# Slots 520 instead of 512 elements long for the streamed operands of a decoder trunk

## The chip, the cores and the metric

The kernel runs on one core of one Trainium2 chip, in one launch. The metric is device time in microseconds. TensorE (PE) multiplies, VectorE (DVE), ScalarE (ACT) and GpSimd (POOL) do the elementwise work, and SyncE (SP) issues most of the loads. All operands of the products lie in SBUF, in tiles of 128 partitions. A place in SBUF is told below by its byte within a partition, as the built program has it, because every partition of a tile uses the same one.

## The reference

Two decoder layers on 1024 tokens of width 1024, all in float32. Cut to what matters:

```python
for i in range(2):
    shift_t, scale_t, gate_t, shift_c, scale_c, gate_c = split(silu(c) @ ada_w[i] + ada_b[i], 6)
    h = rmsnorm(x, norm_g[i, 0]) * (1.0 + scale_t) + shift_t
    y = gla_mixer(h, ...) if i == 0 else diff_mixer(h, ...)      # projections of h, mixing, @ w_o
    x = x + gate_t * y
    h = rmsnorm(x, norm_g[i, 1]) * (1.0 + scale_c) + shift_c
    x = x + gate_c * (square(relu(h @ mlp_w1[i])) @ mlp_w2[i])   # 1024 -> 4096 -> 1024
return rmsnorm(x, final_g)
```

Layer 0 mixes with gated linear attention (4 heads), layer 1 with differential softmax attention (8 heads).

## The kernel before

Activations are held transposed: 8 tiles of 128 features by 1024 tokens, and the tokens in two halves of `HT` = 512. Every float32 operand of a large product is kept as two parts, `hi` (rounded to float32r) and `lo` (the rest), made by `split` (L111). A product of two such operands is three matmuls on PE, in `mm3` (L115 to L118): weight hi with activation hi, weight hi with activation lo, weight lo with activation hi. In most products the weight part is the loaded operand (128 x 128, LDWEIGHTS in the trace, engine row PEld) and the activation part streams through, 512 columns at a time:

```python
pe.matmul(out=o, lhsT=lh, rhs=rh, start=start, stop=False)     # L116
pe.matmul(out=o, lhsT=lh, rhs=rl, start=False, stop=False)     # L117
return pe.matmul(out=o, lhsT=ll, rhs=rh, start=False, stop=stop)  # L118
```

`lhsT` is loaded, `rhs` streams. The streamed tiles that this document is about are these:

- `h`, the input of a projection or of the MLP, in the pool `hp`, which has 16 slots for each of two tags: `hhi` for the first parts (`h_hi`) and `hlo` for the second (`h_lo`). Before the first projection the same slots hold `xn` and `xT`, the input with tokens along the row.
- `hd`, the squared ReLU inside the MLP, in the pool `hid`, with four tags (`hd00`, `hd01`, `hd10`, `hd11`: half of the tokens, then first or second part) of four slots each.

The MLP is in `stretch`: for each of eight chunks of 512 inner features, 8 row groups (two halves of the tokens by four tiles of features) of 24 matmuls stream `h` into PSUM tiles `acc`, `hd` is made from them, and 192 matmuls stream `hd` into `acc` again, whose sums go to the residual `x` on DVE (L712). In the last chunk the second half is done in two pieces of 256 columns. In the MLP of layer 0, called the first MLP below, POOL also loads pieces of the adaLN weights of layer 1, DVE multiplies them, and PE adds them up with four transposes (L220) between two row groups; the MLP of layer 1, the second, has none of this. The output projections stream `h` as well (`acc`, `out_proj`), and so do the projections of the gated linear attention (`pq`, `pk` and `pr`). In the projections of the values there (`pv`) and of the whole differential attention (`pp`) the roles are swapped: a slice of `h` is loaded, and the weight streams, 256, 272 or 384 columns.

A slot is as long as its tile: 2048 bytes for 512 elements. The pools lie one behind the other, so slots of 2048 bytes keep the distance to a multiple of 256 that the first of them has. As built:

| tile | first byte of the first slot | step | bytes behind a multiple of 256 |
|---|---|---|---|
| weights, first and second parts | 19296, 41056 | 4352 | 96, each slice of them too |
| `h_hi` | 71520 | 2048 | 96 |
| `h_lo` | 104288 | 2048 | 96 |
| `hd` of the first MLP | 180256 | 2048 | 32 |
| `hd` of the second MLP | 153440 | 2048 | 96 |

The order of the pools `sm`, `tp`, `xp` and `hid` differs between the layers (`order` in `stretch`), which is why `hd` stands at two different places. The order of the instructions is set by the tile framework's scheduler, and in the two mixers PE's order is written out by hand (an agenda with lags).

Of the kernel before, what the change touches and what calls it, by code (L numbers as in the profile page):

```python
# [10 lines left out]
F32 = mybir.dt.float32  # L11
F32R = mybir.dt.float32r
# [9 lines left out]
P = 128  # L22
D = 1024
T = 1024
KT = D // P
HT = 512
FF = 4096
EPS = 1e-6
# [12 lines left out]

# How much other work of TensorE lies between a piece of work and one that needs its results: in
# rough microseconds of products (gated linear attention), in slots (differential attention).
GLA_LAG = dict(rank=1.09, decay=4.71, keys=3.36, score=4.04, out=7.24, step=2.16, turn=14.56, ada=30.5)
DIFF_LAG = dict(rotary=2.55, keys=1.95, turn=3, next=1.6, value=2, rms=2.66, norm=6.53)
DIFF_END = dict(turn=1.27, next=0.57, value=1.15, rms=1.1, norm=2)
DIFF_LEAD = 22
DIFF_RATE = {True: 2.0, False: 3.0}    # pieces of the output projection per slot, before and after its last operand


class Agenda:
    """Work that is put off until enough other work has been issued (`now` counts it)."""

# [16 lines left out]
def two_pi_parts():  # L70
    """2*pi cut into parts of four bits, so that a part times an integer below 2**20 is exact."""
    rest, parts = 2.0 * math.pi, []
    step = 2.0 ** -1
    while step > 2.0 ** -46:
        part = math.floor(rest / step) * step
        parts.append(part)
        rest -= part
        step /= 16.0
    return [p for p in parts if p]
# [3 lines left out]
def trunk(ctx: ExitStack, tc, a, out):  # L83
    nc = tc.nc
    pe, act, dve, pool = nc.tensor, nc.scalar, nc.vector, nc.gpsimd

# [1 line left out]
    const = ctx.enter_context(tc.tile_pool(name="const", bufs=1))  # L88
# [20 lines left out]

# [1 line left out]
    def split(hi, lo, src):  # L111
# [8 lines left out]
    def weight(src, shape, pinned=False):  # L120
        """Load a piece of a weight and split it into two parts of float32r."""
        raw = wraw.tile(shape, F32, name="raw", tag="raw")
        c0 = 0
        for part in src if isinstance(src, list) else [src]:
            c1 = c0 + part.shape[-1]
            i = nc.sync.dma_start(out=raw[:, :, c0:c1], in_=part)
            c0 = c1
            if pinned:
                in_order(i)
        hi = wsp.tile(shape, F32R, name="whi", tag="whi")  # L130
        lo = wsp.tile(shape, F32R, name="wlo", tag="wlo")
        split(hi, lo, raw)
        return hi, lo

    def wcols(w, c0, n, pinned=False):
        """Columns of a weight with its rows on partitions: [128, k, n]."""
        return weight(w.rearrange("(k p) n -> p k n", p=P)[:, :, c0:c0 + n], [P, KT, n], pinned)
# [5 lines left out]
    def new_half():  # L143
        return [(hp.tile([P, HT], F32R, name="h_hi", tag="hhi"), hp.tile([P, HT], F32R, name="h_lo", tag="hlo"))
                for _ in range(KT)]

    def rsqrt_cols(r, ms, scratch, n, scale=1.0 / D):
        """r = (ms * scale + eps) ** -0.5 for a few columns, with a Newton step."""
        m = scratch.tile([P, n], F32, name="rs_m", tag="rs_m")
        t = scratch.tile([P, n], F32, name="rs_t", tag="rs_t")  # L150
        dve.tensor_scalar(out=m, in0=ms, scalar1=scale, scalar2=EPS, op0=ALU.mult, op1=ALU.add)
        act.activation(out=t, in_=m, func=AF.Ln)
        act.activation(out=r, in_=t, func=AF.Exp, scale=-0.5)
        dve.tensor_tensor(out=t, in0=r, in1=r, op=ALU.mult)
        dve.tensor_tensor(out=t, in0=t, in1=m, op=ALU.mult)
        dve.tensor_scalar(out=t, in0=t, scalar1=-0.5, scalar2=1.5, op0=ALU.mult, op1=ALU.add)
        dve.tensor_tensor(out=r, in0=r, in1=t, op=ALU.mult)

    def broadcast(bc, cols, n):
        """bc[:, j*128:(j+1)*128] = cols[:, j] on every partition."""  # L160
        for j in range(n):
            pe.matmul(out=bc[:, j * P:(j + 1) * P], lhsT=cols[:, j:j + 1].broadcast_to([P, P]),  # L162
                      rhs=ident, start=True, stop=True)

    def norm_mod(x, half, h, gcols, shift, tmp, small, ps, cols=slice(0, HT), on_pool=()):
        """h = x / rms(x) * gcols + shift, in two parts, for the tokens cols of a half."""
        w = cols.stop - cols.start
# [30 lines left out]
    def ada_block(l, c0, n, raws, accs, ps, queue, tag="st", bufs=1):  # L198
        """mod[:, l, c0/128 ...] of n columns: products on VectorE, sum over partitions on PE."""
        ada_sums(l, c0, n, ada_products(l, c0, n, raws, accs, queue), ps, tag, bufs)  # L200
# [25 lines left out]
    def gscale(l, j):  # L226
        """norm_g * (1 + scale) of sub-layer j of layer l."""
        sc = mod[:, l, (3 * j + 1) * KT:(3 * j + 2) * KT]
# [7 lines left out]
    def gla_v(hd, i, pinned=False):  # L236
# [4 lines left out]

# [1 line left out]
    gla = ctx.enter_context(ExitStack())  # L243
    gp = gla.enter_context(tc.tile_pool(name="gp", bufs=1, space=PSUM, reuse_waits="tile"))
    gp2 = gla.enter_context(tc.tile_pool(name="gp2", bufs=1, space=PSUM, reuse_waits="tile"))
    win = a["gla_w_in"][0]
    xn = [hp.tile([P, HT], F32, name="xn", tag="hhi") for _ in range(KT)]
    xT = [hp.tile([P, HT], F32, name="xT", tag="hlo") for _ in range(KT)]
    h = [[(hp.tile([P, HT], F32R, name="h_hi", tag="hhi"), hp.tile([P, HT], F32R, name="h_lo", tag="hlo"))]
         for _ in range(KT)]  # L250

# [115 lines left out]
    def log_sigmoid(z, bias, tp, tag1, tag2):  # L367
        """min(z + b, 0) and log(1 + exp(-|z + b|)); their difference in place of the first."""
        t1 = tp.tile([P, HT], F32, name="ls1", tag=tag1)
# [8 lines left out]
    with gla as g:  # L378
# [49 lines left out]
        def decays(u, first=False):  # L428
            """Cumulated decays of a head inside each tile of 128 tokens, around its middle."""
            hd = u["hd"]  # L430
# [53 lines left out]
        def out_step(u, j):  # L484
            """The outputs of a tile of 128 tokens, and the state behind it."""
            hd, half, v, qi, ks = (u[n] for n in ("hd", "half", "v", "qi", "ks"))
# [46 lines left out]
        def unit(hd, half, ws):  # L533
            """The projections of a head for half of the tokens, in pieces of three products."""
            u = dict(hd=hd, half=half, v=[])
# [45 lines left out]
        with tc.tile_pool(name="xb", bufs=2, reuse_waits="tile") as xb:  # L581
# [7 lines left out]
            def second_half():  # L589
# [5 lines left out]
                for k in range(KT):  # L595
# [5 lines left out]
                    nc.sync.dma_start(out=xs[k, :, HT:T], in_=xc)  # L601
                    hi, lo = hp.tile([P, HT], F32R, name="h_hi", tag="hhi"), hp.tile([P, HT], F32R, name="h_lo", tag="hlo")
                    h[k].append((hi, lo))
# [22 lines left out]
        def stream():  # L626
            """The projections of all heads but the first unit's, and the first ones of the gates."""
            for hd in range(GLA_H):
# [46 lines left out]

# [1 line left out]
    def acc_mm():  # L677
        return mm.tile([P, HT], F32, name="acc", tag="mm")

    def out_proj(h, half, w_o, acc, done, ahead=False, ready=None):  # L680
        """The output projection of a mixer for half of the tokens, in pieces of three products; if
        it is ahead, the last tile of the rows comes at the end, on its own."""
        rows, ends = KT - 1 if ahead else KT, []
# [40 lines left out]
    def stretch(l, h, w_o, ada_todo, after, x=None):  # L724
        with ExitStack() as g:
# [31 lines left out]
            for c in range(FF // 512):  # L757
                ws = [wcols(w1, c * 512 + n * P, P) for n in range(4)]
                hd = [[None, None] for _ in range(4)]
                for half in range(2):  # L760
                    for n in range(4):
# [8 lines left out]
                        dve.tensor_tensor(out=r, in0=r, in1=r, op=ALU.mult)  # L770
                        hd[n][half] = [hid.tile([P, HT], F32R, name="hd", tag=f"hd{half}{i}") for i in range(2)]
                        split(hd[n][half][0], hd[n][half][1], r)
# [37 lines left out]

# [1 line left out]
    win = a["diff_w_in"][0]  # L812
    o = [[None, None] for _ in range(KT)]
    x = [[None, None] for _ in range(KT)]
    with ExitStack() as g:
# [15 lines left out]
        def projections():  # L831
            """The projections of all heads, in pieces of three products."""
            for hd in range(DIFF_H):
# [43 lines left out]
        def turn_qk(hd, half, qk, gi):  # L877
            """Queries as [hi; lo] and keys as [hi; hi] (and lo apart), with dimensions on partitions."""
            tr = dp.tile([P, HT], F32, name="tr", tag="tr", bufs=2)
# [80 lines left out]
        def turn_a(pair, j0):  # L960
            """Weights of two query tiles against two key tiles, with keys on partitions."""
            lastp = j0 == 2 * pair["pr"]
# [115 lines left out]
    def finish(half, cols, x, tp, sm, ps, acc_tile):  # L1078
        """The last norm with tokens on partitions, two tiles of tokens at a time."""
        if not grow:  # L1080
# [39 lines left out]
def diff_constants(tc, const, dc, pos, le, colsT):  # L1120
    """cos and sin of the rotary angles [128 tokens, 8 tiles, 8], -lambda, the sub-norm's gain and
    the causal mask (as an upper bound) of a diagonal block."""
    nc = tc.nc
# [64 lines left out]
```

## Time and profile before

| | before |
|---|---|
| median of 3 runs | 2598.0 us (2597.88 to 2598.4) |
| span of the profiled execution | 2596.7 us |
| PE busy | 2533.6 us, 98% of the span, 12551 matmuls |
| PEld, DVE, ACT, POOL busy | 81%, 57%, 35%, 7% |
| moved by DMA | 202.59 MB, mean 78 GB/s |

The span goes from the first to the last instruction of the one execution that was traced; the runs' own time is taken around the launch and lies 1.3 us above it. A matmul's busy time contains its passage through the array, which overlaps the next matmul, so that the busy times of PE's single instructions add up to more than its share of the span, and the distance from one start to the next is what a matmul costs in a row. Times in the rows below are from the start of the span.

### The profile page before, as it was taken

What the parts mean: (1) busy time and instruction counts of PE and PEld (TensorE: products, weight loads), DVE (VectorE), ACT (ScalarE), POOL (GpSimd) and SP (SyncE); (2) the same over time, 40 slices, a digit from 0 to 9 for tenths busy, and PEclk for the clock granted to TensorE, in tenths of its full rate; (3) what the DMA queues carried; (4) which work ended last, traced back from release to release, by engine and by line L of the source; (5) the groups of instructions that cost most, each with busy time, mean ns of one, the idle gap of its engine ahead of it and who ended that gap; (6) DMA issues with size and microseconds to landing.
All of it is one profiled execution on the core that took longest, in us unless ns stands there. A gap on an engine that the chain in (4) does not pass through costs nothing.

```text
span 2596.7 us, 32374 instructions
## 1 busy us (share of the span) xinstructions
PE 2533.6 (98%) x12551; PEld 2114.2 (81%) x12551; DVE 1481.8 (57%) x2872; ACT 915.4 (35%) x1849; POOL 181.0 (7%) x322
## 2 busy tenths in 40 slices
PE   7899999999999999999999999999999999999998
PEld 5788878888888888888888888887788888888887
DVE  7877786745355445337677777687743343334334
ACT  5645555422112211224455554554422122212222
POOL 2111110001011001000211111110000000000000
PEclk9999999999999999999999999999999999999999
DMA  8333364213133223113001111023311111111111
GB/s 279 120 112 114 119 206 147 81 42 113 50 121 97 93 69 110 41 47 102 25 29 33 34 33 33 23 78 114 114 41 57 41 55 43 50 48 49 49 41 65
DMA packets 224025, 202.59 MB, mean 78 GB/s; under 512 B 10426, under 2 KB 194912, under 8 KB 223872
## 3 DMA queue, kind: packets, MB, share of 16 engines
q1 hardware_dynamic: 209472, 156.33, 19.5%
q0 software_dynamic: 12992, 41.97, 5.2%
q8 instruction: 98, 1.61, 0.3%
q10 hardware_dynamic: 1408, 2.24, 0.2%
q14 instruction: 55, 0.45, 0.1%
HBM read 180.57 MB, written 19.92 MB: 77 GB/s over the span
## 4 chain that ended last, share of the span: by engine, by line
PE 87%; issue 5%; DVE 3%; DMA 2%; ACT 2%; POOL 0%; DVEq 0%; SPq 0%; POOLq 0%; ACTq 0%
PE acc L116 20%; PE acc L117 20%; PE acc L118 20%; PE pp L116 5%; PE pp L118 3%; PE pp L117 3%; DMA ada_raw<-in_ada_w 2%; PE at L966 1%; PE bc L162 1%; PE pr L116 1%; PE pr L117 1%; PE pr L118 1%; PE po L117 1%; PE po L118 1%; PE po L116 1%
## 5 line engine op out<-in xcount | busy, mean ns | idle before, releaser
L116 PE MATMUL acc<-h_hi,whi 128*128 128x512 f32 x1280 | 505.0, 395 | 1.9 <-DVE x L712 1.8
L117 PE MATMUL acc<-h_lo,whi 128*128 128x512 f32 x1280 | 500.5, 391 | 0.0
L118 PE MATMUL acc<-h_hi,wlo 128*128 128x512 f32 x1280 | 500.4, 391 | 0.0
L112 ACT CAST whi<-raw 128x1024 fp32r<-128x1024 f32 (+2 forms) x217 | 221.1, 1020 | 714.3 <-PE acc L117 667.0
L712 DVE SCALAR_TENSOR_TENSOR x<-acc,mod,x 128x512 f32<-128x512 f32 (+1 forms) x312 | 224.2, 722 | 366.4 <-PE acc L118 365.7
L116 PE MATMUL acc<-hd,whi 128*128 128x512 f32 (+1 forms) x1088 | 412.9, 380 | 1.3 <-DVE x L712 1.3
L118 PE MATMUL acc<-hd,wlo 128*128 128x512 f32 (+1 forms) x1088 | 412.7, 379 | 0.0
L117 PE MATMUL acc<-hd,whi 128*128 128x512 f32 (+1 forms) x1088 | 412.3, 379 | 0.0
L113 DVE TENSOR_TENSOR wlo<-raw,whi 128x1024 fp32r<-128x1024 f32 (+2 forms) x217 | 258.5, 1192 | 132.7 <-ACT whi L112 125.7
L116 PEld LDWEIGHTS acc<-h_hi,whi 128*128 128x128 f32 x1280 | 240.9, 188 | 55.2 <-issue 3.6
L118 PEld LDWEIGHTS acc<-h_hi,wlo 128*128 128x128 f32 x1280 | 241.2, 188 | 50.3
L117 PEld LDWEIGHTS acc<-h_lo,whi 128*128 128x128 f32 x1280 | 241.2, 188 | 47.9
L116 PEld LDWEIGHTS acc<-hd,whi 128*128 128x128 f32 x1088 | 204.5, 188 | 42.5 <-DVE x L712 1.8
L118 PEld LDWEIGHTS acc<-hd,wlo 128*128 128x128 f32 x1088 | 204.4, 188 | 40.7
L117 PEld LDWEIGHTS acc<-hd,whi 128*128 128x128 f32 x1088 | 204.3, 188 | 40.7
L770 DVE TENSOR_TENSOR relu<-relu 128x512 f32<-128x512 f32 x128 | 88.0, 688 | 206.0 <-ACT relu L769 205.9
L116 PE MATMUL pp<-whi,h_hi 128*128 128x384 f32 x512 | 199.4, 389 | 0.0
L118 PE MATMUL pp<-whi,h_lo 128*128 128x384 f32 x512 | 172.9, 338 | 0.0
L117 PE MATMUL pp<-wlo,h_hi 128*128 128x384 f32 x512 | 172.5, 337 | 0.0
L769 ACT ACTIVATE relu<-acc 128x512 f32<-128x512 f32 x128 | 75.8, 593 | 219.9 <-PE acc L118 219.9
L207 POOL DMA_DIRECT2D ada_raw<-in_ada_w x160 | 85.9, 537 | 867.0 <-DVE ada_acc L210 531.9
L112 ACT CAST hd<-relu 128x512 fp32r<-128x512 f32 x128 | 79.4, 621 | 158.3 <-DVE relu L770 158.2
(1760 smaller groups left out, 3806.5 us busy)
## 6 DMA issues: line engine op xcount, KB each, us to landing
raw<-in_mlp_w SPq DMA_DIRECT2D x128, 512.0 KB, 3.6
ada_raw<-in_ada_w POOLq DMA_DIRECT2D x160, 256.0 KB, 3.3
raw<-in_gla_w_in SPq DMA_DIRECT2D x24, 512.0 KB, 4.0
raw<-in_diff_w_in SPq DMA_DIRECT2D x64, 192.0 KB, 2.9
raw<-in_diff_w_o SPq DMA_DIRECT2D x17, 512.0 KB, 3.7
aw<-in_ada_w SPq DMA_DIRECT2D x16, 512.0 KB, 7.6
raw<-in_gla_w_o SPq DMA_DIRECT2D x16, 512.0 KB, 3.9
x<-xs SPq DMA_DIRECT2D x32, 256.0 KB, 4.6
```

The source lines that it names most:

```text
L112: act.copy(out=hi, in_=src)
L113: dve.tensor_tensor(out=lo, in0=src, in1=hi.bitcast(F32), op=ALU.subtract)
L116: pe.matmul(out=o, lhsT=lh, rhs=rh, start=start, stop=False)
L117: pe.matmul(out=o, lhsT=lh, rhs=rl, start=False, stop=False)
L118: return pe.matmul(out=o, lhsT=ll, rhs=rh, start=False, stop=stop)
L162: pe.matmul(out=bc[:, j * P:(j + 1) * P], lhsT=cols[:, j:j + 1].broadcast_to([P, P]), rhs=ident, start=True, stop=True)
L207: queue.dma_start(out=w, in_=a["ada_w"][l].rearrange("(k p) n -> p k n", p=P)[:, k:k + kk, c0:c0 + n])
L712: return dve.scalar_tensor_tensor(out=t, in0=psum, scalar=mcols(l, gate)[:, kt:kt + 1], in1=t, op0=ALU.mult, op1=ALU.add)
L769: act.activation(out=r, in_=pt, func=AF.Relu)
L770: dve.tensor_tensor(out=r, in0=r, in1=r, op=ALU.mult)
L966: pe.transpose(out=at[:, n * P:(n + 1) * P], in_=pair["es"][i][:, j * P:(j + 1) * P], identity=ident)
```

## The change

The slots with tag `hhi` and the slots of `hd` become 520 elements (2080 bytes) long. The tiles in them are still 512 wide: the last eight elements are never read or written. The slots of `h_lo` stay at 2048 bytes.

```diff
+PAD = 8
...
     def new_half():
-        return [(hp.tile([P, HT], F32R, name="h_hi", tag="hhi"), hp.tile([P, HT], F32R, name="h_lo", tag="hlo"))
-                for _ in range(KT)]
+        return [(hslot(F32R, "h_hi", "hhi"), hslot(F32R, "h_lo", "hlo")) for _ in range(KT)]
+
+    def hslot(dt, name, tag):
+        return hp.tile([P, HT + (PAD if tag == "hhi" else 0)], dt, name=name, tag=tag)[:, :HT]
...
-                        hd[n][half] = [hid.tile([P, HT], F32R, name="hd", tag=f"hd{half}{i}") for i in range(2)]
+                        hd[n][half] = [hid.tile([P, HT + PAD], F32R, name="hd", tag=f"hd{half}{i}")[:, :HT] for i in range(2)]
```

Three other places that take tiles of these tags (`xn`, `xT`, the first and the second half of layer 0's `h`) call `hslot` in the same way. Comments and docstrings are dropped too, which only shifts line numbers.

As built, consecutive slots of `h_hi` and `hd` now lie 2080 bytes apart, so each is 32 bytes further behind a multiple of 256 than the one before it, and the sixteen slots of a pool take all eight places twice:

| tile | first byte of the first slot | step | bytes behind a multiple of 256 |
|---|---|---|---|
| weights | 19296, 41056 | 4352 | 96 |
| `h_hi` | 71520 | 2080 | 96, 128, 160, 192, 224, 0, 32, 64, and again |
| `h_lo` | 104800 | 2048 | 96 |
| `hd` of the first MLP | 180768 | 2080 | 32, 64, 96, 128, 160, 192, 224, 0, and again |
| `hd` of the second MLP | 153952 | 2080 | 96, 128, 160, 192, 224, 0, 32, 64, and again |

What lies behind `h_hi` in SBUF moves up by 512 bytes, and what lies behind `hd` by another 512, so every other tile keeps its place relative to a multiple of 256.

The instructions and their order are the same, row for row, on all five engines. Three instructions wait for something else than before, all of them on ACT in the second MLP: of the casts that make `hd`, two of the first six now wait for POOL as well as for DVE, and a later one no longer does.

## Rows read from the trace of the kernel before

**Rows 1.** The page: its first line and the busy times.
```profile
span 2596.7 us, 32374 instructions
...
PE 2533.6 (98%) x12551; PEld 2114.2 (81%) x12551; DVE 1481.8 (57%) x2872; ACT 915.4 (35%) x1849; POOL 181.0 (7%) x322
```

**Rows 2.** The page: the chain that ended last, by engine and by line.
```profile
PE 87%; issue 5%; DVE 3%; DMA 2%; ACT 2%; POOL 0%; DVEq 0%; SPq 0%; POOLq 0%; ACTq 0%
PE acc L116 20%; PE acc L117 20%; PE acc L118 20%; PE pp L116 5%; PE pp L118 3%; PE pp L117 3%; DMA ada_raw<-in_ada_w 2%; PE at L966 1%; PE bc L162 1%; PE pr L116 1%; PE pr L117 1%; PE pr L118 1%; PE po L117 1%; PE po L118 1%; PE po L116 1%
```

**Rows 3.** Groups by line and shape on PE; columns as on the page.
```profile
L116 PE MATMUL acc<-h_hi,whi 128*128 128x512 f32 x1280 | 505.0, 395 | 1.9 <-DVE x L712 1.8
...
L116 PE MATMUL acc<-hd,whi 128*128 128x512 f32 x960 | 376.3, 392 | 0.0
...
L118 PE MATMUL pp<-whi,h_lo 128*128 128x384 f32 x512 | 172.9, 338 | 0.0
L117 PE MATMUL pp<-wlo,h_hi 128*128 128x384 f32 x512 | 172.5, 337 | 0.0
...
L116 PE MATMUL pr<-h_hi,whi 128*128 128x512 f32 x128 | 50.8, 397 | 0.0
...
L116 PE MATMUL acc<-hd,whi 128*128 128x256 f32 x128 | 36.6, 286 | 1.3 <-DVE x L712 1.3
...
L116 PE MATMUL pq<-h_hi,whi 128*128 128x512 f32 x64 | 26.4, 413 | 0.1
...
L116 PE MATMUL pk<-h_hi,whi 128*128 128x512 f32 x64 | 25.4, 396 | 0.0
```

**Rows 4.** Timeline of PE, first MLP, series on hd: start us, us, what.
```profile
547.00 0.40 PE L116 MATMUL acc<-hd,whi 128*128 128x512 f32 x1
...
591.56 0.39 PE L118 MATMUL acc<-hd,wlo 128*128 128x512 f32 x1
```

**Rows 5.** Groups by shape on PE, from 546.99 to 591.57.
```profile
L116 PE MATMUL acc<-hd,whi 128*128 128x512 f32 x64 | 25.2, 394 | 0.0
```

**Rows 6.** Timeline of PE, second MLP, a series on hd.
```profile
1925.29 0.39 PE L116 MATMUL acc<-hd,whi 128*128 128x512 f32 x1
...
1968.58 0.39 PE L118 MATMUL acc<-hd,wlo 128*128 128x512 f32 x1
```

**Rows 7.** Timeline of PE, second MLP, the next series, on h.
```profile
1968.81 0.39 PE L116 MATMUL acc<-h_hi,whi 128*128 128x512 f32 x1
...
2012.10 0.39 PE L118 MATMUL acc<-h_hi,wlo 128*128 128x512 f32 x1
```

**Rows 8.** Timeline of PE, first MLP, a series on h.
```profile
681.13 0.39 PE L116 MATMUL acc<-h_hi,whi 128*128 128x512 f32 x1
...
708.13 0.40 PE L118 MATMUL acc<-h_hi,wlo 128*128 128x512 f32 x1
```

**Rows 9.** Windows: length, busy (count) of PE, PEld, DVE, ACT, POOL; clock, DMA.
```profile
547.00:591.00 44.00, 44.00 (x190) 35.34 (x189) 17.37 (x21) 5.30 (x6) 0.00 (x0) 1.00 0.15 45
636.40:680.40 44.00, 44.00 (x190) 35.33 (x189) 22.68 (x30) 5.24 (x6) 4.82 (x9) 1.00 0.35 107
1925.30:1969.30 44.00, 44.00 (x196) 36.47 (x195) 17.71 (x22) 5.76 (x7) 0.00 (x0) 1.00 0.16 49
```

**Rows 10.** Timeline of PE, last chunk of the first MLP, 256 columns.
```profile
1194.47 0.28 PE L116 MATMUL acc<-hd,whi 128*128 128x256 f32 x1
...
1195.94 0.28 PE L117 MATMUL acc<-hd,whi 128*128 128x256 f32 x1
...
1200.36 0.28 PE L117 MATMUL acc<-hd,whi 128*128 128x256 f32 x1
...
1203.77 0.28 PE L116 MATMUL acc<-hd,whi 128*128 128x256 f32 x1
```

**Rows 11.** Timeline of PE, first MLP, series on h behind adaLN transposes.
```profile
625.32 0.48 PE L116 MATMUL acc<-h_hi,whi 128*128 128x512 f32 x1
...
636.11 0.39 PE L118 MATMUL acc<-h_hi,wlo 128*128 128x512 f32 x1
```

More of the change, by code (lines that the diff above doesn't have):

```diff
@@ L246, in trunk @@
     win = a["gla_w_in"][0]
[L247 to L250, printed above, removed]
+    xn = [hslot(F32, "xn", "hhi") for _ in range(KT)]
+    xT = [hslot(F32, "xT", "hlo") for _ in range(KT)]
+    h = [[(hslot(F32R, "h_hi", "hhi"), hslot(F32R, "h_lo", "hlo"))] for _ in range(KT)]
     def token_rms(xt, scratch, ssq, rstd, junk):
@@ L601, in second_half @@
                     nc.sync.dma_start(out=xs[k, :, HT:T], in_=xc)
-                    hi, lo = hp.tile([P, HT], F32R, name="h_hi", tag="hhi"), hp.tile([P, HT], F32R, name="h_lo", tag="hlo")
+                    hi, lo = hslot(F32R, "h_hi", "hhi"), hslot(F32R, "h_lo", "hlo")
                     h[k].append((hi, lo))
```

## The prediction, made before the changed kernel ran

> **What bounds the kernel now.** I read the busy times first. TensorE (PE) is busy for 2533.6 of 2596.7 us; VectorE, the next engine, for 57% of the span [rows 1]. Then the chain that ended last: 87% of it is PE, and its three largest entries are the three products of `mm3`, L116 to L118, into `acc` [rows 2]. So the question is not who waits for whom, but how fast one product follows another. Third, the groups by shape, which say how many products have a slot of the change as their streamed operand [rows 3].
>
> A matmul's own duration (392 ns) is no measure of that, since matmuls overlap. What counts is the spacing of starts, and I take it from the first and the last start of long unbroken series. In the first MLP, one series of 192 products streams `hd`: 64 on each of the three lines [rows 5], first start 547.00, last 591.56 [rows 4]; 44.56 / 191 = 233.3 ns. In the second MLP the same series runs from 1925.29 to 1968.58 [rows 6]: 43.29 / 191 = 226.65 ns. The next one there, 192 products that stream `h_hi` and `h_lo`, gives 43.29 / 191 = 226.65 ns too [rows 7]. Back in the first MLP, 120 products on `h` take 27.00 / 119 = 226.9 ns [rows 8].
>
> So one product of equal shape costs 6.67 ns more in one place: `hd` of the first MLP. Its surroundings do not explain it. The `h` products between those series run at the fast spacing, and the slow series holds 190 products in 44 us whether or not POOL issues its loads and VectorE does 30 pieces of work in place of 21 [rows 9]. What does set `hd` of the first MLP apart is its address: 32 bytes behind a multiple of 256, where every other tile here stands at 96.
>
> The difference is a step. At the granted clock of 1.00 in these stretches [rows 9], the level of 2.4 GHz, 512 columns last 213.3 ns if one passes in a cycle. 226.67 is that plus 13.33, and 233.33 is that plus 20.0: two and three steps of 6.67 ns, each as long as 16 columns, which are 64 bytes of a slot. Products of 256 columns show one step: 14 starts from 1194.47 to 1195.94 give 1.47 / 13 = 113.1 ns against 106.7 [rows 10]. Every streamed operand on L116 to L118 starts 32 bytes off a multiple of 64 (96 and 32 alike), so each touches one 64-byte piece more than its length needs, 33 pieces for 512 columns. My reading: one step is that extra piece; the remaining one or two come from what else is read at the time, such as the next weights, and they depend on where the two streams stand.
>
> The Trainium skill, "TensorE: Matmul & The Clock Gate", section "Back-to-back issue gap", gives N/2.4 + 2.5 ns, 215.8 for 512 columns. The trace disagrees by 10.9 ns in its best series; if the 2976 products counted below as aligned fell to the page's figure, the estimate would be 32 us less.
>
> **The change part by part.** Nothing is added or removed on any engine; three casts to `hd` on ScalarE gain or lose a wait for POOL. They sit in the second MLP, where POOL has nothing to do [rows 9], so I cost them at nothing; if that cover were gone, one late cast would hold back one of eight row groups, whose products are the next to be late.
>
> What moves is addresses. Products with a moved slot as streamed operand, 512 columns wide [rows 3]:
> - `h_hi`, on L116 and L118: 2 x 1280 into `acc`, 2 x 128 into `pr`, 2 x 64 into each of `pq` and `pk`: 3072. `h_lo` keeps its place relative to 256 bytes.
> - `hd`, on all three lines: 3 x 960 = 2880, half in each MLP (1440).
>
> That is 5952 products, and with 16 slots over eight places each place takes an eighth. Half the places are multiples of 64 (0, 64, 128, 192 behind a multiple of 256): 2976 products. For these no row exists. Bounds for one of them: below, 220.0 ns (the fast series less one step); above, 233.3 ns (no benefit, and the slower of the two seen). I take one step off whatever the place would otherwise cost, because the shortest series here are each at least one step above their columns and none is aligned. For the other half the bounds are the two series themselves, 226.67 and 233.33; neither is nearer, since two of the eight places are known and they differ, so I take the middle, 230.0. An aligned place then costs 230.0 - 6.67 = 223.33, and the mean over eight places is 226.67.
>
> The sum:
> - `hd`, first MLP: 1440 x (226.67 - 233.33) = -9.6 us.
> - `hd`, second MLP: 1440 x (226.67 - 226.67) = 0.
> - `h_hi`: 3072 x 0 = 0.
>
> Each nanosecond stays on the path, as PE stands still almost nowhere: 1.9 us before the 1280 products of the first group [rows 3]. The 384 narrower products on `hd` (256 columns, [rows 3]) ran at 113.1 and, after an interruption and at the same addresses, at (1203.77 - 1200.36) / 29 = 117.6 ns [rows 10]; I take 0 and keep 384 x 4.5 = 1.7 us either way. `h_hi` is also the loaded weight of 1024 `pp` products; the streamed operand there is an unmoved weight tile, and the groups with `h_hi` and `h_lo` loaded average 337 and 338 ns [rows 3], so 0; a step in half of them is the bound, 512 x 6.67 = 3.4 us either way. VectorE and ScalarE write the moved slots; they are busy 17 and 5 us of 44 in these series [rows 9], which hides any slower write.
>
> Together -9.6 us: 2596.7 becomes 2587.1 in the profile. The median of the runs lies 1.3 us above the profiled span, so 2588.4; I say 2588.
>
> **The rivals.**
>
> *No benefit from multiples of 64.* The step is a fixed cost of a product, and the places simply mix. With 230.0 everywhere: `hd` of the first MLP gains 1440 x 3.33 = 4.8, that of the second loses 4.8, and `h_hi` loses 3072 x 3.33 = 10.2: +10.2, 2608. This is the case on the other side. Its mechanism is that `h_hi` and the second `hd` give up the best place that the rows show. It decides once the mean over places passes 226.67 + 9.6 / 5.952 = 228.3 ns, that is, once more than two of eight places are slow and none is better. For it: after a disturbance (the sums of the adaLN columns) products at the good place lose it for a while, 48 of them taking (636.11 - 625.32) / 47 = 229.6 ns [rows 11], so the good spacing also hangs on how one product hands over to the next, and `h_hi`, `h_lo`, `h_hi` would now stand at different places. Against it: it leaves the common excess of every width unexplained.
>
> *Only a few places are slow.* With one, two or three slow places of eight and no gain on 64: means of 227.5, 228.33 and 229.17 give 5.952 x (mean - 228.28) = -4.6, +0.3 and +5.3 us. This is no change within what a measurement of this kernel can tell, 0.2% or 5.2 us.
>
> *The place has nothing to do with it.* The 6.67 ns belong to the first MLP's `hd` for another reason, and the time stays 2598. The like count of products with and without that work speaks against it [rows 9]. The Trainium skill, "SBUF — State Buffer", section "Specifications (TRN2)", names cachelines of 16 bytes; by that rule every place before and after is equally good, as all are multiples of 32, and the sum would be 0. The two series [rows 4, 6] disagree with it.
>
> *A larger gain.* Unaligned places cost 226.67 and aligned ones 220.0, mean 223.33: 1440 x 10 + (1440 + 3072) x 3.33 = 29.4 us less, 2568.6. It needs the place 32 to be the only bad one.
>
> **How the numbers follow.** My forecast, a gain of 5 to 20 us by the aligned half: 0.40. The larger gain: 0.05. Few slow places, or no effect of the place: 0.24, of which a little ends as faster. Mixing at a loss: 0.31. So faster 0.46, within 0.2% 0.24, slower 0.30. The range takes in -9.6 with its bounds of 1.7 and 3.4 and half of the way to the larger gain at its lower end, 2574, and the mixing case with a little more than half a microsecond above it, 2609. The forecast's own range is 2577 to 2593.
>
> **What would show it.** If I am right, starts in `hd` series of the first MLP fall from 233.3 to near 226.7 on average, with products whose slot is a multiple of 64 visibly closer to the next (about 220 to 224) than their neighbours; 256-column products may touch 107. If places only mix, the second MLP's series slow to about 230 and no product of 512 columns starts under 225 ns before the next. The second MLP alone separates the two: it holds no adaLN work, and its series are exact to 0.1 ns now. The prediction is wrong if the good spacing needs equal places of consecutive operands, which would cost the `h` products most, or if the step is not 64 bytes of the slot.

## The result, and the profile after

The changed kernel takes 2621.21 us (median of 4 runs, 2619.54 to 2622.99) against 2597.94 us before (4 runs, 2596.03 to 2598.4). The ratio is 1.009, with an interval of 1.0075 to 1.0104: slower by about 23 us. The forecast was 2588, the range 2574 to 2609.

The page of the changed kernel, first its span and busy times, then the chain by engine:

```profile
span 2621.2 us, 32375 instructions
...
PE 2557.1 (98%) x12551; PEld 2115.1 (81%) x12551; DVE 1482.0 (57%) x2872; ACT 915.7 (35%) x1849; POOL 181.8 (7%) x322
...
PE 86%; issue 5%; DVE 3%; DMA 3%; ACT 2%; POOL 0%; SPq 0%; DVEq 0%; ACTq 0%; POOLq 0%
```

Against [rows 1] the span has grown by 24.5 us and PE's busy time by 23.5, while every other engine stands where it was and the chain is still PE's [rows 2]. No new wait shows. The products come more slowly. PE's groups by line and shape (L117 to L119 are the lines L116 to L118 of before):

```profile
L117 PE MATMUL acc<-h_hi,whi 128*128 128x512 f32 x1280 | 510.0, 398 | 2.0 <-DVE x L715 1.8
L118 PE MATMUL acc<-h_lo,whi 128*128 128x512 f32 x1280 | 505.3, 395 | 0.0
...
L117 PE MATMUL acc<-hd,whi 128*128 128x512 f32 x960 | 377.6, 393 | 0.0
```

The idle time before the products is the same to 0.1 us [rows 3], so this is spacing and no wait. `h_lo`, whose slots keep their place, has grown like `h_hi`, which stood at 505.0 [rows 3]; the group of `h_lo` in the kernel before:

```profile
L117 PE MATMUL acc<-h_lo,whi 128*128 128x512 f32 x1280 | 500.5, 391 | 0.0
```

The series that answer to [rows 4, 6, 7], in the timeline of PE: `hd` of the first MLP, `hd` of the second, `h` of the second, 192 products each.

```profile
554.09 0.39 PE L117 MATMUL acc<-hd,whi 128*128 128x512 f32 x1
...
598.27 0.40 PE L119 MATMUL acc<-hd,wlo 128*128 128x512 f32 x1
...
1936.20 0.39 PE L117 MATMUL acc<-hd,whi 128*128 128x512 f32 x1
...
1980.34 0.39 PE L119 MATMUL acc<-hd,wlo 128*128 128x512 f32 x1
1980.57 0.39 PE L117 MATMUL acc<-h_hi,whi 128*128 128x512 f32 x1
...
2024.93 0.39 PE L119 MATMUL acc<-h_hi,wlo 128*128 128x512 f32 x1
```

44.18 / 191 = 231.3 ns where 233.3 was, 44.14 / 191 = 231.1 where 226.65 was, and 44.36 / 191 = 232.3 where 226.65 was. One row group of the second series, product by product:

```profile
1936.88 0.39 PE L117 MATMUL acc<-hd,whi 128*128 128x512 f32 x1
1937.12 0.39 PE L118 MATMUL acc<-hd,whi 128*128 128x512 f32 x1
1937.34 0.40 PE L119 MATMUL acc<-hd,wlo 128*128 128x512 f32 x1
1937.58 0.39 PE L117 MATMUL acc<-hd,whi 128*128 128x512 f32 x1
...
1938.27 0.39 PE L117 MATMUL acc<-hd,whi 128*128 128x512 f32 x1
```

The group of three from 1936.88 stands at 128, 0 and 128 behind a multiple of 256, all multiples of 64, and lasts 0.70 us; the one from 1937.58 stands at 160, 32 and 160, none a multiple of 64, and lasts 0.69 us. A row group is four such groups of three. Averaged over the whole series, the two that start on multiples of 64 take 693.4 and 694.4 ns, the other two 692.4 and 693.0. A start on a multiple of 64 buys nothing.

Summing the distances from each start to the next over both whole traces, kind by kind, gives where the 24.5 us went: +20.1 on the 4608 products on `h` (about a third of it on `h_lo`), +6.4 on the 512-column products on `hd` of the second MLP, -2.8 on those of the first, +0.8 on all else.

### The profile page after: what moved, and what is told of

Same layout as the page of the kernel before. It is cut to its first block, busy times and chain, and to the rows that moved or that the text cites. A ratio compares the mean times of both kernels' runs of the same rounds, so it can differ in the third digit from the quotient of the medians.

```text
span 2621.2 us, 32375 instructions
## 1 busy us (share of the span) xinstructions
PE 2557.1 (98%) x12551; PEld 2115.1 (81%) x12551; DVE 1482.0 (57%) x2872; ACT 915.7 (35%) x1849; POOL 181.8 (7%) x322
## 4 chain that ended last, share of the span: by engine, by line
PE 86%; issue 5%; DVE 3%; DMA 3%; ACT 2%; POOL 0%; SPq 0%; DVEq 0%; ACTq 0%; POOLq 0%
PE acc L117 20%; PE acc L118 20%; PE acc L119 20%; PE pp L117 4%; PE pp L119 3%; PE pp L118 3%; DMA ada_raw<-in_ada_w 2%; PE at L969 1%; PE pr L118 1%; PE pr L117 1%; PE pr L119 1%; PE bc L166 1%; PE po L118 1%; PE po L119 1%; PE po L117 1%
## 5 line engine op out<-in xcount | busy, mean ns | idle before, releaser
L117 PE MATMUL acc<-h_hi,whi 128*128 128x512 f32 x1280 | 510.0, 398 | 2.0 <-DVE x L715 1.8
L118 PE MATMUL acc<-h_lo,whi 128*128 128x512 f32 x1280 | 505.3, 395 | 0.0
L119 PE MATMUL acc<-h_hi,wlo 128*128 128x512 f32 x1280 | 504.8, 394 | 0.0
L117 PE MATMUL acc<-hd,whi 128*128 128x512 f32 (+1 forms) x1088 | 414.0, 381 | 1.4 <-DVE x L715 1.3
L119 PE MATMUL acc<-hd,wlo 128*128 128x512 f32 (+1 forms) x1088 | 413.6, 380 | 0.0
L118 PE MATMUL acc<-hd,whi 128*128 128x512 f32 (+1 forms) x1088 | 413.4, 380 | 0.0
L117 PEld LDWEIGHTS acc<-h_hi,whi 128*128 128x128 f32 x1280 | 240.4, 188 | 60.9 <-issue 3.6
L119 PEld LDWEIGHTS acc<-h_hi,wlo 128*128 128x128 f32 x1280 | 240.9, 188 | 56.6
L118 PEld LDWEIGHTS acc<-h_lo,whi 128*128 128x128 f32 x1280 | 240.8, 188 | 53.7
L117 PEld LDWEIGHTS acc<-hd,whi 128*128 128x128 f32 x1088 | 204.3, 188 | 43.6 <-DVE x L715 1.8
L119 PEld LDWEIGHTS acc<-hd,wlo 128*128 128x128 f32 x1088 | 204.4, 188 | 41.8
L118 PEld LDWEIGHTS acc<-hd,whi 128*128 128x128 f32 x1088 | 204.3, 188 | 41.7
L117 PE MATMUL pp<-whi,h_hi 128*128 128x384 f32 x512 | 199.7, 390 | 0.0
L118 PE MATMUL pp<-wlo,h_hi 128*128 128x384 f32 x512 | 172.9, 338 | 0.0
L119 PE MATMUL pp<-whi,h_lo 128*128 128x384 f32 x512 | 172.8, 337 | 0.0
```

## The experiments

All begin from the kernel before unless it is said otherwise. Whole pools are moved by a tile that nobody uses, and behind the pool a second gap brings the rest of SBUF back to its place relative to a multiple of 256:

```diff
+    def gap(stack, n):
+        if n:
+            stack.enter_context(tc.tile_pool(name=..., bufs=1)).tile([P, n], F32, name="gap")
```

The mm3 lines are L126 to L128 in these kernels (L127 to L129 in `e11_second_weights_64_on`). Spans are compared with the 2596.7 us of before. Most experiments ran once, and 17 runs of the kernel before span 2591.8 to 2598.6 us, so a difference of a few us in one span says little; the spacing within most series repeats to 0.1 ns. The theory after the result: the spacing of products is set by **the place** of the streamed slot modulo 256 bytes, absolute or relative to the weights. Its rivals: the spacing belongs to **the stage**; or a product pays for **the jump** from the place of the one before it.

**The first MLP's `hd` at 96** (`e1_first_mlp_at_96`)

```diff
                 if n == "hid":
+                    gap(g, 16 if l == 0 else 0)      # 64 bytes
```

> The kernel before, with a gap of 64 bytes ahead of the slots of hd in the first MLP, so that all streamed operands of the two MLPs stand 96 bytes behind a multiple of 256, as the weights do. If the address sets the spacing of products (each place has a price, or only equal places with the weights are cheap), the 1440 products on hd of the first MLP fall from 233.3 to 226.7 ns and the span from 2596.7 to about 2587 us. If the slow spacing belongs to the first MLP's surroundings and not to the address, the spacing stays 233.3 and the span 2597.

Measured: 2588.07 us (5 runs) against 2597.18 for the kernel before on the same chip, ratio 0.9969, interval 0.9955 to 0.9983; span 2586.4. The series on `hd` of the first MLP, timeline of PE:

```profile
548.68 0.39 PE L126 MATMUL acc<-hd,whi 128*128 128x512 f32 x1
...
591.98 0.39 PE L128 MATMUL acc<-hd,wlo 128*128 128x512 f32 x1
```

43.30 / 191 = 226.7 ns. A gap of 64 bytes takes the whole 6.67 ns away. The stage is out.

**Everything streamed at 32** (`e2_all_at_32`): a gap of 192 bytes ahead of `hp` and ahead of the second MLP's `hid`.

> The kernel before, with h_hi, h_lo and the second MLP's hd shifted as whole pools, so that every slot of h and hd stands 32 bytes behind a multiple of 256 and consecutive slots are all alike, while the weights stay at 96. If the price hangs on the place itself (or on its distance to the weights' place), every product of 512 columns costs 233.3 ns, as the first MLP's hd does: 6.67 ns on 4608 products on h and 1440 on hd, +40 us, span about 2637. If only differences between consecutive streamed operands cost something, the products on h keep 226.7 and the span stays near 2597.

Measured: 2626.45 us, span 2624.7. The series on `h` of the second MLP:

```profile
1979.94 0.40 PE L126 MATMUL acc<-h_hi,whi 128*128 128x512 f32 x1
...
2024.51 0.39 PE L128 MATMUL acc<-h_hi,wlo 128*128 128x512 f32 x1
```

44.57 / 191 = 233.35 ns, and `hd` gives the same, as the place theory says; all slots are alike here, so jumps between slots are not needed for the loss. The span grew by 28.0 and not by 40, although the long series of the second MLP lose the full 6.67 ns per product. In the first MLP part of `h` did not run at the fast spacing before either [rows 11] and had less to lose, but that is only 0.9 us. More of it has nothing to do with places: the mixer of layer 1 is 2.9 us shorter than before, and the stretch just ahead of the second MLP's long series 3.0 us. That stretch, first in the kernel before, then in this run (length, then busy times, granted clock, DMA):

```profile
1876.90:1925.20 48.30, 45.63 (x197) 37.76 (x196) 27.08 (x41) 19.35 (x30) 0.00 (x0) 0.93 0.19 59
...
1889.80:1935.10 45.30, 43.93 (x197) 35.53 (x196) 26.83 (x41) 18.19 (x29) 0.00 (x0) 1.00 0.19 59
```

The granted clock was 0.93 there before and is 1.00 here. In the kernel before PE stood idle for 2.67 us in it, and for some microseconds after that its 512-column products start 0.43 us apart, which is the level of 1.2 GHz; here it was idle for 1.37 us and the products behind it start 0.23 us apart. From the kernel before:

```profile
1879.93 1.84 PE L179 MATMUL st<-ones_col,sq 128*128 128x1 f32 x8 [2.67 <-DVE sq L175]
...
1883.05 0.63 PE L117 MATMUL acc<-h_lo,whi 128*128 128x512 f32 x1
1883.48 0.63 PE L118 MATMUL acc<-h_hi,wlo 128*128 128x512 f32 x1
```

Spans hold such differences; the long series do not.

**The two halves of the change** (`e3_pad_hd_only`, `e4_pad_h_only`): the diff above for `hid` alone, and for `hp` alone.

> The change for hd alone; h stays as before. Place theory and hand-over theory (a product pays for standing at another place than the one before it) agree that hd shows what the full change showed, 231.4 ns in the first MLP and 231.2 in the second, net +3.5 us, span about 2600; the products on h keep 226.7 in the second MLP.

> The change for h_hi alone; hd stays as before. If each place has its own price, the products on h_hi slow as in the full change (+13 us) and those on h_lo, whose place does not change, keep 226.7 in the second MLP: span about 2610. If a product pays for the place of its neighbours, those on h_lo slow too (to about 232 ns, +6.6 us): span about 2617. In both cases hd stays at 233.3 in the first MLP and 226.7 in the second.

Measured: spans 2601.4 and 2613.7, that is +4.7 and +17.0, together 21.7 of the 24.5. With `hd` padded alone, its series show 231.3 and 231.1 ns, and `h` of the second MLP 226.9. With `h_hi` padded alone, the series on `h` of the second MLP:

```profile
1978.06 0.39 PE L126 MATMUL acc<-h_hi,whi 128*128 128x512 f32 x1
...
2022.41 0.39 PE L128 MATMUL acc<-h_hi,wlo 128*128 128x512 f32 x1
```

44.35 / 191 = 232.2 ns over all three lines, with `h_lo` included, whose place has not changed: from the start of a product on `h_lo` to the next start it is 233.4 ns. So a product's cost does not hang on its own slot alone: the simple place theory fails for `h_lo`.

**The weights at 32** (`e5_weights_at_32`): a gap of 192 bytes ahead of `wsp`, undone behind `wraw`.

> The kernel before with the weights' pools moved to 32 bytes behind a multiple of 256; h and the second MLP's hd stay at 96 and the first MLP's hd at 32. If the spacing hangs on the place of the streamed slot itself, nothing changes: 233.3 ns for hd of the first MLP, 226.7 for the rest, span 2597. If it hangs on the distance between streamed slot and weights, hd of the first MLP, now at the weights' place, falls to 226.7 (-9.6 us), and h and the second MLP's hd, now 64 bytes ahead of the weights, take a value that no run has shown yet.

Measured: 2600.89 us, span 2599.2. First a series on `hd` of the first MLP (at 32, as before), then one on `hd` of the second (at 96, as before):

```profile
639.92 0.40 PE L126 MATMUL acc<-hd,whi 128*128 128x512 f32 x1
...
683.26 0.39 PE L128 MATMUL acc<-hd,wlo 128*128 128x512 f32 x1
...
2009.63 0.39 PE L126 MATMUL acc<-hd,whi 128*128 128x512 f32 x1
...
2053.35 0.39 PE L128 MATMUL acc<-hd,wlo 128*128 128x512 f32 x1
```

43.34 / 191 = 226.9 ns where 233.3 was, and 43.72 / 191 = 228.9 where 226.65 was. No streamed slot has moved relative to 256, and the spacings have changed over: it is the distance between streamed slot and weights that counts, not the place. The two reads do go on at the same time: in the kernel before, a weight load starts with the stream of the product ahead of its own.

```profile
1925.74 0.39 PE L118 MATMUL acc<-hd,wlo 128*128 128x512 f32 x1
...
1925.74 0.19 PEld L116 LDWEIGHTS acc<-hd,whi 128*128 128x128 f32 x1
```

**The other distances** (`e6_places_128_192_224`, `e7_places_160_64_0`): gaps ahead of `hp` and of each `hid`, weights at 96.

> The kernel before with whole pools shifted: h_hi and h_lo at 128 bytes behind a multiple of 256, hd of the first MLP at 192, hd of the second at 224, all slots of a pool alike, weights at 96. If starts on a multiple of 64 are cheaper by one step, as the prediction had it, h (128) and the first hd (192) go to 220 ns, or at least below the second hd (224). If they are not, each place has its own value between 226.7 and 235, and none is under 226.7.

> As the run before, with h at 160, hd of the first MLP at 64, hd of the second at 0. Multiples of 64 cheaper: both hd series at 220 to 223 ns and h above them. Not cheaper: all between 226.7 and 235. With the two runs all eight places are known, and their mean says how much of the change's loss the places alone explain: a mean near 231.5 explains all of it, a mean near 228 leaves the rest to the jumps between places.

Measured: 2636.18 us (span 2634.4) and 2616.47 (2614.7). From the first, a series on `hd` of the first MLP, at 192:

```profile
648.40 0.39 PE L126 MATMUL acc<-hd,whi 128*128 128x512 f32 x1
...
692.96 0.39 PE L128 MATMUL acc<-hd,wlo 128*128 128x512 f32 x1
```

44.56 / 191 = 233.3 ns. From the second, two series on `h` in the second MLP, both at 160:

```profile
1969.41 0.39 PE L126 MATMUL acc<-h_hi,whi 128*128 128x512 f32 x1
...
2013.13 0.39 PE L128 MATMUL acc<-h_hi,wlo 128*128 128x512 f32 x1
...
2148.11 0.40 PE L126 MATMUL acc<-h_hi,whi 128*128 128x512 f32 x1
...
2192.68 0.40 PE L128 MATMUL acc<-h_hi,wlo 128*128 128x512 f32 x1
```

228.9 ns and, with the same slots 135 us after that series ended, 44.57 / 191 = 233.35, the price of most other distances. All distances, from series of 192 products in these runs, in bytes by which the streamed slot stands ahead of the weights modulo 256:

| distance | 0 | 32 | 64 | 96 | 128 | 160 | 192 | 224 |
|---|---|---|---|---|---|---|---|---|
| ns | 226.7 | 233.3 | 228.9 or 233.3 | 233.3 | 233.3 | 234.3 | 233.3 | 233.3 |

Only distance 0 is cheap, and neither starts on multiples of 64 (distances 32, 96, 160 and 224 here) nor the others are under it. The mean over all eight, with 231.1 for 64, is 232.3.

**`h_lo` 128 bytes away from `h_hi`** (`e8_lo_128_off`): the version with all at 96, a gap of 128 bytes between the two tags of `hp`.

> The version with all operands of the MLPs at 96, but h_lo shifted to 224, so that each product on h_lo stands 128 bytes away from the products on h_hi around it, all slots of a kind alike. If each place has its own price, the products on h_hi keep 226.7 ns and only those on h_lo (1536 of 4608) change, to the value that 224 shows as a place of its own. If the jump costs, the products on h_hi slow too, and h as a whole goes to about 231 ns, +20 us on 2587.

Measured: 2595.91 us, span 2594.2, +7.8 on the version it starts from. Outside the stretch where the clocks of the two runs differ, the products on `h` lost about 11 us. From the second chunk of each MLP on, the price stays with the product that is off: in the second MLP the mean distance from a start to the next is 234.2 ns for `h_lo` and 226.7 and 225.8 for `h_hi`'s two products, 228.9 over all three. But in the second half of layer 0's output projection and in the first chunk of each MLP, all three are slow and the mean is 233.7 or 233.8, with slots at the same places. So a jump of 128 bytes before and behind every `h_lo` costs little more than the distance itself in most series, and as much as the jump theory says in some. Jumps as the main cause do not fit: the loss is about half of the 20 us, and `e2_all_at_32` loses without any jump.

**Everything at distance 0, on multiples of 64** (`e9_all_at_128`): gaps of 32 bytes ahead of `wsp` and `hp`, of 96 and 32 ahead of the two `hid`.

> Weights, h and hd of both MLPs all moved to 128 bytes behind a multiple of 256, so that streamed slots and weights stand at the same distance (0) as in the version with all at 96, and every slot starts on a multiple of 64. If only the distance between streamed slot and weights counts, the products of 512 columns cost 226.7 ns, the span is about 2587 and the median about 2588. If a start on a multiple of 64 saves a step of 6.67 ns, as the prediction had it, they cost 220 ns, and 7488 of them make the span about 50 us shorter, 2537.

Measured: 2584.58 us (5 runs) against 2596.12 before, ratio 0.9957, interval 0.9942 to 0.9971; span 2585.9. A series on `hd` of the first MLP:

```profile
637.64 0.39 PE L126 MATMUL acc<-hd,whi 128*128 128x512 f32 x1
...
680.94 0.39 PE L128 MATMUL acc<-hd,wlo 128*128 128x512 f32 x1
```

43.30 / 191 = 226.7 ns, as at 96. The prediction's 64-byte step does not show. This version and the one with all at 96 beat both kernels, and their intervals overlap.

**Longer slots without other places, and 16 bytes** (`e10_step_2304_and_16_bytes`): from the version with all at 96, 64 more elements to each slot of `hd`, and the tile cut out as `[:, 4 * l:4 * l + HT]`.

> The version with all at 96, with slots of hd 2304 bytes long instead of 2048, so that the step is a multiple of 256 and all keep one place; in the second MLP the tile starts 16 bytes into its slot, at 112. If the change's loss comes from the places and not from longer slots, hd of the first MLP stays at 226.7 ns. For the second MLP: if the good place is one narrow point, its hd goes towards 233; if it is as wide as 32 bytes, it stays at 226.7.

Measured: 2595.42 us, span 2593.7. `hd` of the first MLP stays at 226.7 ns, so the length of a slot costs nothing, and places that differ by a multiple of 256 are alike. `hd` of the second, 16 bytes off:

```profile
2003.41 0.39 PE L126 MATMUL acc<-hd,whi 128*128 128x512 f32 x1
...
2047.66 0.40 PE L128 MATMUL acc<-hd,wlo 128*128 128x512 f32 x1
```

44.25 / 191 = 231.7 ns. The good point is narrower than 16 bytes on this side.

**The second weight parts 64 bytes on** (`e11_second_weights_64_on`): from the version with all at 96, a gap of 64 bytes between the two tags of `wsp`.

> The version with all at 96, but the second weight parts (wlo) at 160; first parts, h and hd stay at 96. While L117's product streams, wlo is loaded for L118's; while L116's and L118's stream, whi is loaded. If the cost arises between a stream and the load that runs at the same time, only the products on L117 go to 233 (their stream stands 64 bytes behind the load), and about 2496 x 6.6 = 16 us are lost. If it arises from a product's own weights, the products on L118 slow instead. If the loads don't matter, nothing changes and the span is 2587.

Measured: 2614.58 us, span 2612.9. The series on `hd` show 231.1 ns on average. By line, the mean distances from a start to the next in them are 228.3, 229.2 and 235.8, and the groups of PE by line and shape show the same order in the durations:

```profile
L129 PE MATMUL acc<-hd,wlo 128*128 128x512 f32 x960 | 381.5, 397 | 0.0
L128 PE MATMUL acc<-hd,whi 128*128 128x512 f32 x960 | 376.3, 392 | 0.0
L127 PE MATMUL acc<-hd,whi 128*128 128x512 f32 x960 | 373.5, 389 | 0.0
```

Neither branch of what was expected came out. The product with the displaced weights of its own (L129) is slowest, but the two others are slower than 226.7 as well; three products cost 693.3 ns in place of 680, two steps of 6.67 more. Which of the two reads waits for the other is not told apart by this.

**Another order of the three products** (`e12_change_order_hi_hi_lo`): the changed kernel, with

```diff
-        pe.matmul(out=o, lhsT=lh, rhs=rl, start=False, stop=False)
-        return pe.matmul(out=o, lhsT=ll, rhs=rh, start=False, stop=stop)
+        pe.matmul(out=o, lhsT=ll, rhs=rh, start=False, stop=False)
+        return pe.matmul(out=o, lhsT=lh, rhs=rl, start=False, stop=stop)
```

> The changed kernel with the second and the third product of each group of three exchanged, so that the same streamed slot stands in two successive products and the place changes twice instead of three times in a group of three on h. If the change's loss is that of the places alone, the span stays near 2620. If jumps between places cost something of their own, it falls by several us.

Measured: 2618.64 us, span 2616.9, 4.3 under the changed kernel's. The series on `h` of the second MLP stay at 232.2 ns and those on `hd` at 231.2; `hd` of the first MLP falls from 231.3 to 230.1, 1.9 us. The rest is not traced to any series, and four runs of the changed kernel span 2617.8 to 2621.2 us, so 4.3 is hardly clear of their scatter. This leaves a small cost of jumps open, and no large one.

## Why the prediction was wrong

- **What bounds the kernel: right.** The change moved no work; nearly all of the 24.5 us are spacing of products on PE, and the three moved waits of ScalarE cost nothing that the trace shows. The terms put at nothing, the products of 256 columns and `pp`, lie in the +0.8 us of all else.
- **The address sets the spacing of the first MLP's `hd`: right.** 64 bytes of gap turn 233.3 into 226.7 ns, 9.6 us over its 1440 products; the span falls by 10.3.
- **"One step is that extra piece": the step that failed.** It took one step of 6.67 ns off the 2976 products on multiples of 64, 19.8 us in all, and so turned a loss into a gain. With everything on multiples of 64 and distance 0 the spacing is 226.7, the same as off them. That all shortest series stood at least one step above their columns was no evidence, as no row had an aligned start to set against them. I wrote that no row existed for them and still took the step off every one.
- **"Neither is nearer, so I take the middle, 230.0": mis-sized.** Two known places of eight, one good and one bad, were treated as an even split. At 232.3 in place of 230.0 the 5952 moved products cost 13.7 us more. Both readings of the rows, absolute place and distance to the weights, fitted them; I took the place, although I had written that the steps "depend on where the two streams stand". By distance, `h`, the second `hd` and the weights all standing at 96 would have been the special case, equality, and the first `hd` the ordinary one. The seven other distances measure 228.9 to 234.3, and the mean over all eight is 232.3.
- **`h_lo` "keeps its place", and the sum has no term for it: wrong.** Its products, at distance 0 throughout, take 233.5 ns from their start to the next in the second MLP's series, more than the 231.9 and 231.3 of the products on moved slots. In all it is 6.9 us.
- One sum beside the argument is wrong: 2976 products from the 223.33 ns of the estimate to 215.8 are 22 us, not 32, which counts from 226.67. Nothing else uses it.

With the measured mean the prediction's own sum reads: 3072 x 5.66 = 17.4 for `h_hi`, 1440 x 5.66 = 8.15 for the second `hd`, 1440 x (232.3 - 233.3) = -1.4 for the first, together +24.1 against 24.5 measured. That the total fits is luck, for its parts do not: `h_hi` lost 13.2, the second `hd` 6.4, the first gained 2.8, and `h_lo` makes up for it. A product does not simply pay for its own distance. In the second MLP's series on `hd`, the group of three at 96, 224 and 96 has two products at distance 0 and would take 2 x 226.7 + 233.3 = 686.7 ns by the table, as it does in most series of `e8_lo_128_off`; it takes 692.4, as the other groups do. On `h`, each half of the tokens has one group with all three slots at distance 0, and no group there takes less than 685 ns, where 680 is the price with everything at distance 0.

The mixing rival had the sign and the mechanism, and under half of the size, because it took 230.0. Its signs were those that came: the second MLP's series slowed, to 231.1 and 232.3 where it said about 230, and none of their products starts less than 225 ns before the next.

What is shown: where all slots of a series are alike, the spacing hangs on the distance between streamed operand and weights, with one cheap value. What stays open is how the two reads get in each other's way, why the cost spreads to neighbours, and why distance 64, and `h_lo` 128 bytes off, have two values with the same slots. The Trainium skill, "TensorE: Matmul & The Clock Gate", section "Step-by-step: what each phase is for", gives the streamed operand and the weight load independent read ports, so that "Loading the next tile's weights doesn't steal SBUF read bandwidth from the running matmul". By that one would not expect the weights' place to matter to the stream; `e5_weights_at_32` shows that it does, 226.9 against 233.3 ns.

## What to carry to other kernels

Where PE is bound by back-to-back products in float32r, compute the first byte of the streamed operand and of the weights modulo 256 before touching anything else, and make them equal by whole gaps ahead of pools; here that gave 0.3 to 0.4%. The gain shows in products of 512 columns; the 192 of 256 columns in the first MLP gained nothing by the move from 32 to 96 (+0.2 us). A slot length that is no multiple of 256 bytes spreads the slots over places of which most are bad, and the products beside them pay too. When two measured points fit two rules (a place, a distance), price the change by both before choosing, and ask which of the two points is the ordinary one.

## What was not expected of the hardware

- Moving only the weights' tiles by 192 bytes, with no streamed tile moved relative to 256, changed the spacing of the 512-column products on them: 233.3 to 226.9 ns on `hd` of the first MLP, 226.65 to 228.9 on `hd` and `h` of the second.
- 16 bytes between the streamed slot's place and the weights' cost 5.0 ns of 226.7 per product.
- The same slots at distance 64 ran at 228.9 ns in one series and at 233.3 in later ones of the same execution.
- Between products at other distances, products at the weights' own place lost the cheap spacing: `h_lo`, never moved, took 233.5 ns where it had taken 226.7.
